# Three steps of the mixers issued later, six small tables loaded through GpSimd's queue

## The chip, the cores and the metric

One core of one Trainium2 chip runs the whole program in one launch. The metric is device time in microseconds, the median of repeated runs. TensorE (PE) does the matrix products, VectorE (DVE) and ScalarE (ACT) the elementwise work, GpSimd (POOL) a smaller share of it; SyncE (SP) issues nearly all the loads.

## What is computed

A decoder trunk of two layers over 256 positions of width 1024, in float32. Each layer runs four causal token mixers (retention, Mamba-2 SSD, gated linear attention, mLSTM) on the same normalised input, whose inputs all come from one wide projection. The four results are gated, merged and projected back. Then comes a channel mixer: a dense SwiGLU in layer 0, two of eight experts in layer 1.

```python
for l in range(DEPTH):
    h = rmsnorm(x, mix_norm_g[l])
    x = x + token_mixers(h, pos, w_in[l], ...)      # four mixers, gates, merge, w_out
    h = rmsnorm(x, ffn_norm_g[l])
    x = x + (swiglu(h, w1, w3, w2) if l % 2 == 0 else moe_ffn(h, router_w, w1, w3, w2))
return rmsnorm(x, final_norm_g)

# in token_mixers
u = h @ w_in                                        # sz, sxbc, sdt, gq, gk, gv, ga, mqk, mv, mi, mf, ...
xbc = silu(causal_dwconv(sxbc, ssd_conv_w, ssd_conv_b))     # SSD: x, B, C after a convolution
dt = softplus(sdt + ssd_dt_bias); a = -exp(ssd_a_log)       # SSD: scores are C @ B^T times decays of dt * a
alpha_pre = ga @ gla_w_alpha + gla_b_alpha                  # GLA: the rate product
m_t = maximum(inter, max(dlog))                             # mLSTM: a running maximum of the gate sums
```

## The kernel before

**Weights and cuts.** Each weight is read from memory once, in loads of 1 MB that SP issues (`fetch`, L270). A load is cut in two halves; each half is split in a high part (ScalarE, `hi`, L296) and a low part (VectorE, `lo`, L297), and three float32r products per tile (L302 to L304, `mm3`) stand for one float32 product. A half of a load is 24 matmuls of 256 columns, or 12 of 512. TensorE can start on a half when its `lo` is done. The order of the loads in a mixer stage is: z with the narrow columns, three of SSD's `xbc`, two of mLSTM's `mqk`, two of `mv`, then GLA, retention, gates, branches and the output.

**Side chains.** Everything between the projections is written as Python generators (`Side`), one per chain: `narrow` (rates, cumulative sums and mLSTM's maximum), `gla_decays`, `ssd`, `mlstm` and so on. The kernel keeps a modelled clock, `now`, which each `mm3` moves on by about 322 ns. After each `mm3`, `tick` steps every chain that is due. `yield n` makes a chain due again 1500 * n ns later, `yield 0` 700 ns later. So a `yield` sets after how many projection matmuls the chain's next instructions are issued, on every engine that they use.

**Orders.** The emission gives the priority; the framework's own scheduler makes each engine's queue from it, and only in the first norm and the z load of layer 0 are VectorE and ScalarE held to the written order. An engine works its queue in order: a TensorE instruction that waits holds up every projection matmul behind it.

**The tables.** `load_tables` (L353) is called once, after the first three weight loads. SP loads constants (L356, L357), five row tables (L360 to L364), five tables of eight numbers broadcast to all partitions (`bc`, L367), `walpha` (L369) and the router weights (L375). `ic`, `z` and `ea` in `narrow` (L677 to L686) read `bc`; GLA's rate product (L751) reads `walpha`.

**GLA's rate product.** `gla_decays` transposes its 16 narrow columns (L745), copies them out of PSUM (`gaT`, L748), multiplies by `walpha` (L751) and goes on to the decays; 9 us of the modelled clock after their scan it issues two exponentials on ScalarE (L776) over what GpSimd computes at L772 and L773.

**SSD.** `ssd` waits in emission for the convolutions of `xbc2` and `xbc4` (their last instruction is L578) and then issues the score products (L522, L523 from L980).

**mLSTM's maximum.** `narrow` scans the rows on VectorE (`mrow`, L726) and transposes the result on TensorE (L730).

**After the mixers.** Layer 0's SwiGLU follows in the same manner. Layer 1 ends with the experts, whose weights are loaded in 2 MB pieces (`quad`, L265) into buffers that exist only when the mixers' buffers have been given back.

Of the kernel before, what the change touches and what calls it, by code (L numbers as in the profile page):

```python
# [23 lines left out]
L = 2  # L24
# [78 lines left out]
def _bcast(ap, dims):  # L103

    return bass.AP(tensor=ap.tensor, offset=ap.offset, ap=[[0, P]] + dims)
# [36 lines left out]
class Trunk:  # L142
# [210 lines left out]
    def load_tables(self):  # L353
        nc, a = self.nc, self.a
        n0 = C_OFFS["ident"][1]
        nc.sync.dma_start(self.keep[:, n0:], a["consts"][:, n0:C_KEEP])  # L356
        nc.sync.dma_start(self.mixk[:, :C_LATE - C_KEEP], a["consts"][:, C_KEEP:C_LATE])  # L357
        rows = self.mixc.tile([102, P], F32, name="rows")
        r = lambda n, pat: a[n].rearrange(pat, p=P)
        nc.sync.dma_start(rows[0:48], r("ssd_conv_w", "l k (b p) -> (l k b) p"))  # L360
        nc.sync.dma_start(rows[48:60], r("ssd_conv_b", "l (b p) -> (l b) p"))
        nc.sync.dma_start(rows[60:92], r("ml_conv_w", "l k (b p) -> (l k b) p"))
        nc.sync.dma_start(rows[92:100], r("ml_conv_b", "l (b p) -> (l b) p"))
        nc.sync.dma_start(rows[100:102], r("gla_b_alpha", "l (b p) -> (l b) p"))  # L364
        self.bc = self.mixc.tile([P, 5, L, 4], F32, name="bc")
        for i, n in enumerate(("ssd_dt_bias", "ml_b_i", "ml_b_f", "ssd_a_log", "ssd_d")):
            nc.sync.dma_start(self.bc[:, i], _bcast(a[n], [[4, L], [1, 4]]))  # L367
        self.walpha = self.mixc.tile([16, L, P], F32, name="walpha")
        nc.sync.dma_start(self.walpha, a["gla_w_alpha"].rearrange("l r c -> r l c"))  # L369
        self.rows = rows  # L370
        self.ranks = self.const.tile([P, 2 * P], F32R, name="ranks")
        for i, n in enumerate(("tris", "ones")):
            nc.gpsimd.tensor_scalar(self.ranks[:, i * P:(i + 1) * P], self.c(n), 1.0, None, op0=OP.mult)
        self.rw = self.const.tile([P, KT, NE], F32, name="rw")
        nc.sync.dma_start(self.rw, a["router_w"][0].rearrange("(k p) e -> p k e", p=P))  # L375
# [205 lines left out]
    def mixers(self, l):  # L581
        nc, a, tc = self.nc, self.a, self.tc
# [19 lines left out]
        def wait(name):  # L602

            while name not in sides or not sides[name].done:
                yield 1
# [40 lines left out]
        def out_tile():  # L646
            po = self.psum()
            return po.rearrange("p (t h d) -> p t h d", t=2, h=4)
# [13 lines left out]
        def narrow():  # L662
# [7 lines left out]
            if l == 0:  # L670
                self.turn_tables()
            add_side("gla", gla_decays())
            for t in range(2):
                yield from silu2(szs[:, t], pz[t][:, :256])
# [49 lines left out]
            crow, mrow = [T((4, S), n_, 2, tag="row") for n_ in ("crow", "mrow")]  # L724
            nc.vector.tensor_copy(crow, pr[:4, :S])
            nc.vector.tensor_tensor_scan(mrow, crow, crow, 0.0, op0=OP.max, op1=OP.max)  # L726
            yield 1
            pm = self.psum()
            for t in range(2):
                nc.tensor.transpose(pm[:, t * 4:t * 4 + 4], mrow[:, t * P:(t + 1) * P], ident[:4, :4])  # L730
# [9 lines left out]
        def gla_decays():  # L740

            sm = G["sm"]
            pga = self.psum()
            for t in range(2):
                nc.tensor.transpose(pga[:16, t * P:(t + 1) * P], sm[:, t, 12:28], ident)  # L745
            yield 1
            gaT = T((16, S), "gaT", 2, tag="row")
            nc.vector.tensor_copy(gaT, pga[:16, :S])  # L748
            yield 0
            pal = self.psum()  # L750
            nc.tensor.matmul(pal[:, :S], self.walpha[:, l], gaT, start=True, stop=True)  # L751
            yield 1
            gz, ge, gu = T((P, S), "gz"), T((P, S), "ge"), T((P, S), "gu")
            nb = self.nvec[:, l:l + 1]
            nc.vector.tensor_scalar(gz, pal[:, :S], -1.0, nb, op0=OP.mult, op1=OP.add)
            nc.scalar.activation(ge, gz, AF.Abs)
            nc.scalar.activation(ge, ge, AF.Exp, scale=-1.0)
            yield 0
            nc.vector.tensor_scalar(gu, ge, 1.0, None, op0=OP.add)
            nc.vector.scalar_tensor_tensor(ge, gu, -1.0, ge, op0=OP.add, op1=OP.subtract)  # L760
            nc.scalar.activation(gu, gu, AF.Ln)
            yield 2
            nc.vector.tensor_sub(gu, gu, ge)
            nc.vector.scalar_tensor_tensor(gu, gz, 0.0, gu, op0=OP.max, op1=OP.add)
            nc.vector.tensor_tensor_scan(gz, gu, gu, 0.0, op0=OP.add, op1=OP.bypass)
            G["E"] = E = self.block("E").rearrange("p (n s) -> p n s", s=S)
            for i, s in enumerate(LEVELS):
                gv = gz.rearrange("p (n u s) -> p n u s", u=2, s=s)
                ev = E[:, i].rearrange("p (n u s) -> p n u s", u=2, s=s)
                n = S // (2 * s)  # L770
                ref = gv[:, :, 0, s - 1:s].to_broadcast([P, n, s])
                nc.gpsimd.tensor_tensor(ev[:, :, 0], ref, gv[:, :, 0], op=OP.subtract)  # L772
                nc.gpsimd.tensor_tensor(ev[:, :, 1], gv[:, :, 1], ref, op=OP.subtract)  # L773
            yield 6
            for i in range(0, NL, 4):
                nc.scalar.activation(E[:, i:i + 4], E[:, i:i + 4], AF.Exp, scale=-1.0 / 16.0)  # L776
            yield from gla_scores()
# [184 lines left out]
        def ssd():  # L962
# [12 lines left out]
            nc.gpsimd.tensor_tensor(hv(xdx), hv(xs), bc[:, 4, l, None, :, None].to_broadcast([P, 2, 4, 64]), op=OP.mult)  # L975
            for n in ("xbc2", "xbc4"):
                yield from wait(n)
            o, late = out_tile(), None
            for g in range(2):
                sc = self.scores(xbc[:, 2 + g], xbc[:, 4 + g])  # L980
# [149 lines left out]
        if l == 0:  # L1130
            add(order.close)
        spawn("narrow", narrow)
        for b in (0, 2, 4):
            plan += self.proj_cm(w, C_XBC + b * P, hT, ssd_conv(b))
            if b == 0:
                spawn("ssd", ssd)
# [585 lines left out]
```

## Time and profile before

| what | value |
|---|---|
| runs | 1483.81, 1484.91, 1490.21 us; median 1484.91 |
| profiled execution | 1487.51 us, of which the span is 1485.4 us |
| PE busy | 1384.5 us, 93% of the span |
| PE weight loads | 901.3 us, 61% |
| DVE busy | 612.1 us, 41% |
| ACT busy | 534.7 us, 36% |
| POOL busy | 185.3 us, 12% |
| mean granted TensorE clock | 0.983 of full |
| read from memory | 400.39 MB |

The shares are means over stages that differ: up to about 749 us the core computes two mixer stages and a SwiGLU, after that it streams expert weights. A busy PE isn't PE at its peak. What a change in one stage is worth has to be read from that stage's windows, from the waits and from the timeline around them. Times in rows are microseconds from the span's start unless the row says ns; the last figure in brackets of a timeline row is the idle time before the instruction and what ended it.

### The profile page before, as it was taken

The page shows a single profiled execution, that of the slowest core. Times are in us where ns is not written, and L with a number is a line of the kernel's source. Part 1 is how long each engine was busy: PE and PEld are TensorE (multiplying, and loading weights), DVE is VectorE, ACT ScalarE, POOL GpSimd, SP SyncE. Part 2 cuts the span into 40 slices and gives each one's busy share as a digit, 9 for nine tenths or more (in the row PEclk, how much of TensorE's full clock was granted, in tenths as well). Part 3 has the DMA queues.
Part 4 walks back from the last instruction along what each step waited for, and adds up shares of the span by engine and source line. Part 5 has one row for each costly group of instructions (what it writes and reads, how often), then busy time and mean ns, then how long its engine had stood idle before and what let it go on. Part 6 is the DMA issues. An engine that isn't in the chain of part 4 may idle for free. (4 is left out here: it accounts for less than half of the span.)

```text
span 1485.4 us, 26500 instructions
## 1 busy us (share of the span) xinstructions
PE 1384.5 (93%) x11170; PEld 901.3 (61%) x11170; DVE 612.1 (41%) x1069; ACT 534.7 (36%) x717; POOL 185.3 (12%) x211
## 2 busy tenths in 40 slices
PE   7999999999999999999999999989889998988884
PEld 6888999799998978999974332322223222332221
DVE  5866555654446786565553121221112121212112
ACT  5643444444444643344422322222222222222112
POOL 0366211100000227323110000000000000000000
PEclk9999999999999999999989999999999999999997
DMA  8735366675551433635387999999999999999991
GB/s 251 254 114 156 114 199 208 201 239 189 191 178 57 157 123 105 199 114 182 102 317 279 409 409 408 399 401 408 408 408 408 409 408 408 401 398 408 408 398 64
DMA packets 182474, 404.43 MB, mean 272 GB/s; under 512 B 12470, under 2 KB 95804, under 8 KB 182076
## 3 DMA queue, kind: packets, MB, share of 16 engines
q1 hardware_dynamic: 181612, 400.34, 73.2%
q8 instruction: 93, 1.52, 0.4%
q10 hardware_dynamic: 720, 2.16, 0.4%
q14 instruction: 49, 0.40, 0.1%
HBM read 400.39 MB, written 2.10 MB: 271 GB/s over the span
## 5 line engine op out<-in xcount | busy, mean ns | idle before, releaser
L312 PE MATMUL ps<-quad,X 128*32 128x512 f32 (+1 forms) x3072 | 325.6, 559 | 29.4 <-DMA quad<-in_moe_w_dram 29.1
L297 DVE TENSOR_TENSOR lo<-raw,hi 128x1024 fp32r<-128x1024 f32 x222 | 277.3, 1254 | 167.1 <-ACT hi L296 166.8
L302 PE MATMUL ps<-hThi,hi 128*128 128x256 f32 x1120 | 319.7, 285 | 0.0
L304 PE MATMUL ps<-hTlo,hi 128*128 128x256 f32 x1120 | 314.9, 281 | 0.4 <-DVE hTlo L297 0.4
L303 PE MATMUL ps<-hThi,lo 128*128 128x256 f32 x1120 | 314.9, 281 | 0.0
L296 ACT ACTIVATE hi<-raw 128x1024 fp32r<-128x1024 f32 x222 | 232.9, 1056 | 205.2 <-PE ps L304 114.1
L1511 DVE COPY own<-quad 128x1024 f32 (+1 forms) x140 | 92.7, 663 | 505.6 <-DMA quad<-in_moe_w_dram 439.0
L1512 ACT ACTIVATE own<-quad 128x1024 f32 (+1 forms) x140 | 141.1, 1010 | 443.9 <-DMA quad<-in_moe_w_dram 380.5
L312 PEld LDWEIGHTS ps<-quad,X 128*32 128x32 f32 x3072 | 92.0, 109 | 232.4 <-issue 160.0
L302 PEld LDWEIGHTS ps<-hThi,hi 128*128 128x128 f32 x1120 | 212.4, 190 | 2.9 <-issue 0.7
L303 PEld LDWEIGHTS ps<-hThi,lo 128*128 128x128 f32 x1120 | 211.7, 189 | 0.6
L304 PEld LDWEIGHTS ps<-hTlo,hi 128*128 128x128 f32 x1120 | 211.6, 189 | 0.6 <-DVE hTlo L297 0.6
L312 PE MATMUL ps<-quad,gT 128*32 128x512 f32 x1408 | 160.5, 595 | 28.5 <-DMA quad<-in_moe_w_dram 27.9
L312 PEld LDWEIGHTS ps<-quad,gT 128*32 128x32 f32 x1408 | 41.6, 109 | 143.3 <-issue 84.4
L416 POOL TENSOR_TENSOR rstd<-rs,mhalf 128x1 f32<-128x1 f32 x10 | 5.5, 556 | 932.1 <-DVE rs L412 915.1
L312 PE MATMUL ps<-own,X 128*32 128x512 f32 (+1 forms) x768 | 93.5, 558 | 0.0
L1103 POOL TENSOR_TENSOR m<-m 128x512 f32<-128x512 f32 x16 | 34.8, 2173 | 152.2 <-DVE m L1101 144.8
L312 PEld LDWEIGHTS ps<-own,X 128*32 128x32 f32 x768 | 24.3, 110 | 46.7 <-issue 44.3
L302 PE MATMUL ps<-hi,hThi 128*128 128x512 f32 (+1 forms) x128 | 51.2, 402 | 0.2 <-ACT hi L296 0.2
L304 PE MATMUL ps<-lo,hThi 128*128 128x512 f32 (+1 forms) x128 | 47.9, 375 | 0.4 <-DVE lo L297 0.4
L303 PE MATMUL ps<-hi,hTlo 128*128 128x512 f32 (+1 forms) x128 | 48.2, 377 | 0.0
L312 PE MATMUL ps<-own,gT 128*32 128x512 f32 x352 | 45.9, 593 | 0.0
(332 smaller groups left out, 1483.1 us busy)
## 6 DMA issues: line engine op xcount, KB each, us to landing
quad<-in_moe_w_dram SPq DMA_DIRECT2D x108, 2048.0 KB, 21.3
raw<-in_w_in_dram SPq DMA_DIRECT2D x62, 1024.0 KB, 5.5
quad<-in_moe_w_dram SPq DMA_DIRECT2D x32, 1536.0 KB, 16.8
raw<-in_ffn_w_dram SPq DMA_DIRECT2D x33, 1024.0 KB, 5.3
raw<-in_w_branch_dram SPq DMA_DIRECT2D x8, 1024.0 KB, 5.3
raw<-in_w_out_dram SPq DMA_DIRECT2D x8, 1024.0 KB, 5.0
mixk<-in_consts_dram SPq DMA_DIRECT2D x1, 1536.0 KB, 14.9
x<-in_x_dram SPq DMA_DIRECT2D x2, 512.0 KB, 5.2
```

Of the source, the lines that this page charges most:

```text
L296: nc.scalar.activation(hi, src, AF.Copy)
L297: nc.vector.tensor_sub(lo, src, hi.bitcast(F32))
L302: mm(out, ah, bh, start=start, stop=False)
L303: mm(out, al, bh, start=False, stop=False)
L304: mm(out, ah, bl, start=False, stop=stop)
L312: ins = self.nc.tensor.matmul(outs[gs], a, b, start=start, stop=stop, tile_position=(0, SUB * g))
L416: nc.gpsimd.tensor_tensor(out, v, mh, op=OP.pow)
L1103: nc.gpsimd.tensor_tensor(m[:, 0:2], m[:, 0:2], m[:, 2:4], op=OP.add)
L1511: nc.vector.tensor_copy(own[:, 0:1, :n_], raw[:, bass.ds(v0, 1)])
L1512: nc.scalar.activation(own[:, 1:2, :n_], raw[:, bass.ds(v1, 1)], AF.Copy)
```

## The change

Six loads move from SP's queue to GpSimd's. Three `yield`s change: mLSTM's maximum is transposed one step (1.5 us of the modelled clock) later, GLA's rate product is issued 3.0 us instead of 0.7 us after the copy before it, and a new `yield 4` (6 us) stands between the last convolution of SSD and its scores. No arithmetic changes.

```diff
@@ load_tables
         for i, n in enumerate(("ssd_dt_bias", "ml_b_i", "ml_b_f", "ssd_a_log", "ssd_d")):
-            nc.sync.dma_start(self.bc[:, i], _bcast(a[n], [[4, L], [1, 4]]))
+            nc.gpsimd.dma_start(self.bc[:, i], _bcast(a[n], [[4, L], [1, 4]]))
         self.walpha = self.mixc.tile([16, L, P], F32, name="walpha")
-        nc.sync.dma_start(self.walpha, a["gla_w_alpha"].rearrange("l r c -> r l c"))
+        nc.gpsimd.dma_start(self.walpha, a["gla_w_alpha"].rearrange("l r c -> r l c"))
@@ narrow
             nc.vector.tensor_tensor_scan(mrow, crow, crow, 0.0, op0=OP.max, op1=OP.max)
-            yield 1
+            yield 2
             pm = self.psum()
@@ gla_decays
             nc.vector.tensor_copy(gaT, pga[:16, :S])
-            yield 0
+            yield 2
             pal = self.psum()
             nc.tensor.matmul(pal[:, :S], self.walpha[:, l], gaT, start=True, stop=True)
@@ ssd
             for n in ("xbc2", "xbc4"):
                 yield from wait(n)
+            yield 4
             o, late = out_tile(), None
```

## Rows read from the trace of the kernel before

**Rows 1.** Windows by stage: from:to, length, busy us of PE, PEld, DVE, ACT, POOL, clock, DMA share, GB/s

```profile
13.00:477.00 464.00, 454.06 (x3243) 424.36 (x3244) 279.12 (x415) 213.82 (x284) 88.42 (x94) 0.99 0.57 182
477.00:749.00 272.00, 265.11 (x1914) 248.62 (x1914) 173.21 (x309) 122.28 (x180) 88.29 (x93) 0.98 0.42 134
749.00:1470.00 721.00, 657.17 (x5990) 222.35 (x5988) 152.13 (x330) 192.08 (x242) 5.62 (x14) 0.99 0.98 388
```

**Rows 2.** Waits of PE, whole span: us in total, times, longest us

```profile
PE ps L312 <- DMA quad<-in_moe_w_dram: 57.0, 82, 1.8
...
PE ps L522 <- DVE xbc L578: 6.2, 2, 3.2
PE ps L751 <- DVE gaT L748: 3.1, 1, 3.1
...
PE ps L730 <- DVE mrow L726: 1.1, 2, 0.7
```

**Rows 3.** Timeline of ACT, DVE and PE, 24 to 33 us: start, duration, instruction

```profile
25.34 0.21 ACT L686 ACTIVATE ea<-bc 128x4 f32<-128x4 f32 x1 [4.76 <-DMA bc<-in_ssd_a_log_dram]
...
26.52 1.23 DVE L297 TENSOR_TENSOR lo<-raw,hi 128x1024 fp32r<-128x1024 f32 x1 [2.46 <-ACT hi L296]
...
28.23 0.41 DVE L748 COPY gaT<-ps 16x256 f32<-16x256 f32 x1
...
28.70 0.69 PE L751 MATMUL ps<-gaT,walpha 16*128 16x256 f32 x2 [3.13 <-DVE gaT L748]
...
32.00 1.06 ACT L296 ACTIVATE hi<-raw 128x1024 fp32r<-128x1024 f32 x1 [3.27 <-DMA raw<-in_w_in_dram]
```

**Rows 4.** Timeline of SP's queue, start of the program

```profile
3.15 4.84 SPq L382 DMA_DIRECT2D narrow<-in_w_in_dram  x1
...
19.43 0.36 SPq L367 DMA_DIRECT2D bc<-in_ssd_dt_bias_dram  x1
...
22.03 0.43 SPq L369 DMA_DIRECT2D walpha<-in_gla_w_alpha_dram  x1
...
23.59 8.28 SPq L270 DMA_DIRECT2D raw<-in_w_in_dram  x4
```

**Rows 5.** Windows of a few us, columns as in rows 1

```profile
29.63:33.05 3.42, 3.42 (x18) 3.42 (x17) 2.35 (x13) 1.05 (x2) 0.00 (x0) 0.50 1.09 348
60.35:63.77 3.42, 3.42 (x12) 2.95 (x12) 2.78 (x7) 0.69 (x2) 0.00 (x0) 0.50 0.94 289
524.57:531.39 6.82, 5.67 (x16) 4.76 (x17) 6.12 (x12) 2.68 (x5) 0.00 (x0) 0.50 0.49 154
20.00:25.50 5.50, 5.50 (x47) 5.34 (x46) 2.07 (x7) 0.74 (x3) 1.06 (x2) 1.00 0.07 9
34.00:48.00 14.00, 13.53 (x113) 13.11 (x112) 14.00 (x35) 10.01 (x15) 6.41 (x9) 1.00 1.07 367
```

**Rows 6.** Timeline of ACT, DVE and PE ahead of SSD's scores, layers 0 and 1

```profile
47.95 1.06 ACT L776 ACTIVATE E<-E 128x1024 f32<-128x1024 f32 x1 [3.36 <-POOL E L773]
...
58.33 1.20 DVE L297 TENSOR_TENSOR lo<-raw,hi 128x1024 fp32r<-128x1024 f32 x1
59.46 0.67 DVE L578 SCALAR_TENSOR_TENSOR xbc<-th,xbc 128x512 f32<-128x512 f32 x1
...
60.28 1.13 PE L522 MATMUL ps<-xbc 128*128 128x256 f32 x2 [2.99 <-DVE xbc L578]
...
523.76 1.22 DVE L297 TENSOR_TENSOR lo<-raw,hi 128x1024 fp32r<-128x1024 f32 x1
...
525.73 1.19 PE L522 MATMUL ps<-xbc 128*128 128x256 f32 x2 [3.21 <-DVE xbc L578]
```

**Rows 7.** Timeline of POOL and DVE, start of the program

```profile
1.22 0.11 POOL L888 MEMSET mvv<- 128x16 f32 x1
6.83 0.55 POOL L416 TENSOR_TENSOR rstd<-rs,mhalf 128x1 f32<-128x1 f32 x1 [5.50 <-DVE rs L412]
...
8.14 1.41 DVE L442 SCALAR_TENSOR_TENSOR h<-x,rstd,gain_mix_norm_g 128x512 f32<-128x512 f32 x2 [1.45 <-DMA gain_mix_norm_g<-in_mix_norm_g_dram]
```

## The prediction, made before the changed kernel was run

> **What bounds the kernel now.** I read the windows by stage first. Up to 749 us TensorE is busy nearly all the time (454.1 of 464 us, then 265.1 of 272) while the DMA engines are at 0.57 and 0.42; after it they are at 0.98 and TensorE waits for expert weights [rows 1]. The expert stage starts when the last mixer buffers are free, and its loads set its length; so it keeps its length and moves as a block, and a microsecond that TensorE saves before 749 us should reach the end whole.
>
> Second, TensorE's waits [rows 2]. The 57.0 us for `quad` are the expert stage. What the change can touch is the scores of SSD (6.2 us, once per layer), GLA's rate product (3.1 us, layer 0 alone) and the transpose of mLSTM's maximum (1.1 us over both layers). Third, the timeline around each wait, for who is late, and fourth, short windows behind it for the granted clock.
>
> **What a wait costs besides its length.** Behind the rate product the clock is granted at 0.50, the 1.2 GHz level, for 3.42 us of full work; behind layer 0's scores for 3.42 us; in layer 1 the half-clock stretch runs to 531.39, and TensorE works in it from 525.73 [rows 5, 6]. Before each of them TensorE had stood still for about 3 us. Half of 3.42, 3.42 and 5.66 us are lost: 1.7, 1.7 and 2.8. The two waits for the maximum are short, and I give them no clock loss.
>
> **Part 1, the rate product and the tables.** The chain in layer 0 reads: `ea` on ScalarE waits 4.76 us for a table that SP issued late, the split of a weight half queued behind it starts only then, its `lo` on VectorE at 26.52, `gaT` at 28.23, and L751 on TensorE at 28.70 after 3.13 us idle, with all projection matmuls behind it [rows 3]. Either edit alone cuts this chain. The tables have no input to wait for, so GpSimd, idle from 1.33 to 6.83 us [rows 7], can issue them at once; and L751 comes 2.3 us of the modelled clock later, some 7 `mm3`. Gain: 3.1 + 1.7 = **4.8 us**.
>
> What is late next? The next load must be there. SP issues six tables, the router weights and a gain from 19.43 to 23.59, and then the next four loads [rows 4], while the DMA engines are at 0.07 [rows 5]. Six eighths of these 4.16 us are 3.1 us. The first of the four lands at 32.00, where ScalarE waits for it [rows 3], so then at 28.9; with the split (1.06) and `lo` (1.23) the half is ready at 31.2. TensorE, freed at 25.57, has the rate product (0.6 us) and 48 matmuls at 0.117 us (47 in 5.5 us [rows 5]), 5.6 us, and asks at 31.8: no wait.
>
> On the price of the six tables on SP, the Trainium skill (DMA: Bandwidth & Descriptors, "Issuing engines are not separate DMA queues") says that DMAs of all issuers run on the same 16 engines, and that another issuer saves only the time of issuing. By that, with 0.36 to 0.43 us for each issue [rows 4], the loads would come about 2.4 us earlier instead of 3.1, and the forecast would rise by 0.7; the gaps between these issues speak for the larger figure.
>
> **Cost at the start.** No row shows a DMA issued by GpSimd. Its queue also holds the power (`rstd`, 6.83) of the first norm, and VectorE and TensorE wait for that norm; behind it `h` waits for its gain until 8.14 anyway, 0.76 us after `rstd` ends [rows 7]. So six issues cost nothing if they end by 7.59, that is, up to 1.04 us each. Lower end: 0.36 us each as on SP, cost 0. Upper end: 4.84 us each, the dearest issue on SP [rows 4]: 29.0 us, so `rstd` at 30.4, and 22.8 us lost. No gain is possible here, since x and the gain are what is waited for. These loads are small like the 0.36 us row, so I stay near it, with a margin: 1.13 us each, **0.5 us** lost.
>
> **Part 2, the scores.** The last convolution instruction ends at 60.13, 2.8 us after TensorE ran out at 57.29 [rows 6]. Four steps are 6 us of the modelled clock, 18.6 `mm3`, 56 matmuls, 6.5 us at 0.117. That is twice the wait, in both layers. Gain: 3.0 + 1.7 in layer 0 and 3.2 + 2.8 in layer 1, **10.7 us**. What covers it: the matmuls that move ahead of the scores are those of `mv`, and their halves must be cut by then. Layer 0: TensorE would reach `mv` at 57.3 - 4.8 - 0.5 = 52.0 and its second half one half later (24 matmuls, 2.8 us), at 54.8. That half's `lo` ends at 59.53 [rows 6]. VectorE is busy for all of 34 to 48 us [rows 5], so its work moves up only as far as its start does; I give it the 3.1 us of the loads: 56.4, and TensorE waits 1.6 us. Between 0 (VectorE also gains from the moved scores) and 4.7 (all that was to be won) I take **1.6**. Layer 1: TensorE reaches `mv` 0.65 us earlier than 522.5 and wants its second half at 524.7; the `lo` ends at 524.98 [rows 6], 0.3 us late. But GLA's exponentials, which hold ScalarE up (3.36 us in layer 0 [rows 6]), come up to 2.3 us later too; they may fall behind the splits that they now delay, or delay them longer. Between 0 and 6.0 I take **1.0**. SSD's later steps end before retention's loads force them.
>
> **Part 3, the maximum.** One step is 1.5 us, the waits are 1.1 us in all [rows 2]: gain **1.1 us**. Its reader, mLSTM, waits for `mv` much longer.
>
> **Sum.** 4.8 + 10.7 + 1.1 = 16.6 us won; 0.5 + 1.6 + 1.0 = 3.1 given back; 13.5 net. The profiled execution takes 1487.5 us, 2.1 of them outside its span of 1485.4; it would come to 1474.0. The runs' median is 1484.9, 2.6 below that execution, so I forecast 1484.9 - 13.5 = **1471.4 us**.
>
> **Rivals.**
> *The cuts become the bound.* VectorE was full for 14 us at a stretch [rows 5]; what waited for the scores would wait for `lo` instead, as long and with the same clock loss. The 10.7 us go, 4.8 + 1.1 - 0.5 = 5.4 stay: 1479.5 us. Against it: 0.3 us is all that layer 1 shows.
> *The scores don't move on TensorE.* The `yield`s set the emission, the framework sets the queues; it may put the scores back where they were. Part 1 alone stays, 4.8 - 0.5: 1480.6 us. Against it: these queues follow the emission at every wait in rows 2.
> *The tables come late.* If GpSimd issues them only while VectorE is busy and is slowed by it, `ea` still holds ScalarE and TensorE then waits for the half behind it. Part 1 goes: 1476.2 us. VectorE's first instruction comes after 6 us and GpSimd is free from 1.33 [rows 7], which speaks against it.
> This is the rule in the Trainium skill, SBUF — State Buffer, "SBUF: two separate sides": GpSimd writes the descriptors of its DMAs itself and can't while certain VectorE instructions hold the port that both share. No run so far shows it.
> *Slower: the norm waits behind the tables.* At 4.84 us for each issue the 22.8 us of above are lost at `rstd`, and 1484.9 - 14.0 + 22.8 = 1493.7 us. It decides against the change from (14.0 + 0.76 + 5.50) / 6 = 3.4 us per issue on, nine times the SP row.
>
> **How the numbers follow.** Forecast 0.65 (its own range 1467 to 1477), cuts 0.12, scores don't move 0.10, tables late 0.08, slower 0.05. The low end, 1467, is nearly all of the 16.6 us with 1 us for luck; the high end, 1480, takes in the tables' case and most of the cuts'. About 0.5%, 7.4 us, is what a measurement of this kernel can tell from no change. Faster by more (under 1477.5): 0.63 of the forecast, 0.06 of the tables' case, 0.04 of the cuts': 0.73. Within: 0.21. Slower by more: 0.06, the slow rival and a little for what I don't see.
>
> **What would show it.** Right: no wait at L751, L522 from `xbc` and L730; full clock at 25 to 36, 55 to 66 and 520 to 534 us; the four loads issued at about 20.5; `rstd` before 8 us; the first `quad` load some 13 us earlier, and the expert stage as long as before. A row that waits for `lo` or `hi` in 45 to 60 or 520 to 530 would size parts 1 and 2; `ea` still waiting, the tables' case. Wrong would be an expert stage that takes back what was won, or a first TensorE product of the z load after 15 us.

## The result, and the profile of the changed kernel

The changed kernel takes **1492.97 us** (median of 11 runs, 1491.42 to 1496.26); the kernel before takes 1484.15 (11 runs beside them). The ratio is 1.0058, with a 95% interval of 1.0045 to 1.0070: slower by 0.6%, where 1471.4 and a range of 1467 to 1480 stood in the forecast. The profiled execution takes 1493.46 us with a span of 1491.3. From L978 on, lines of the changed kernel stand one higher than before; L442 to L842, which are named most, are the same lines.

The waits of TensorE over the whole span come first (us in total, times, longest), beside [rows 2]:

```profile
...
PE ps L452 <- DVE h L442: 13.2, 4, 9.0
PE ps L842 <- POOL bd L827: 5.3, 2, 2.8
PE ps L522 <- DVE xbc L578: 2.7, 2, 2.2
PE ps L710 <- issue: 2.7, 1, 2.7
PE ps L531 <- DVE as L988: 1.8, 2, 1.1
...
PE ps L802 <- POOL ge L791: 0.6, 1, 0.6
...
PE ps L730 <- DVE mrow L726: 0.3, 1, 0.3
```

The three waits that the change aimed at are nearly gone: L751 from 3.1 us to none, L522 from 6.2 to 2.7, L730 from 1.1 to 0.3. In their place stand 9.0 us at L452, the first norm's transposes; 2.7 at L710, the sums of the rates; 5.3 at L842, GLA's products, which wait for a masked copy (`bd`) made by GpSimd; and smaller ones at L531 and L802. So 7.4 us of waits went, and some 15 came (L452 had 7.4 us before, L842 1.1). The page names no releaser for L710. Its operand is `rates`, whose last write on VectorE ends just ahead of it:

```profile
40.50 0.17 DVE L705 COPY rates<-sp 128x8 f32<-128x8 f32 x1
...
40.77 0.36 PE L710 MATMUL ps<-rates,mixk 128*128 128x8 f32 x2 [2.73 <-issue]
```

The start, from the timelines of GpSimd, ScalarE, SP's queue and TensorE:

```profile
1.31 0.80 POOL L367 DMA_DIRECT2D bc<-in_ssd_dt_bias_dram  x1
...
4.22 0.56 POOL L369 DMA_DIRECT2D walpha<-in_gla_w_alpha_dram  x1
...
12.84 0.57 POOL L416 TENSOR_TENSOR rstd<-rs,mhalf 128x1 f32<-128x1 f32 x1 [7.94 <-DVE rs L412]
...
11.48 0.20 ACT L686 ACTIVATE ea<-bc 128x4 f32<-128x4 f32 x1 [5.54 <-DMA bc<-in_ssd_a_log_dram]
11.60 0.61 ACT L421 ACTIVATE junk<-x 128x512 bf16<-128x512 f32 x1
...
4.08 7.34 SPq L382 DMA_DIRECT2D narrow<-in_w_in_dram  x1
...
24.30 8.41 SPq L270 DMA_DIRECT2D raw<-in_w_in_dram  x4
...
14.25 1.97 PE L452 MATMUL ps<-keep,h 128*128 128x128 f32 x8 [8.99 <-DVE h L442]
```

GpSimd's issues are cheap, 0.56 to 0.80 us, and over by 4.8. But the framework has now put `ea`, which stood at 25.34 before [rows 3], between the squares of `x` on ScalarE, and there it waits until its table lands, 8.3 us after that table's issue. The written order to which ScalarE is held at the start begins behind these squares, which are emitted with the load of `x`, and ends ahead of `ea`; so it doesn't keep the two apart. `rstd` therefore comes at 12.84 instead of 6.83 [rows 7], and not for the reason that the slower rival gave, since GpSimd's issues were over 8 us earlier. SP's second narrow load needs 7.34 us where it needed 4.84 [rows 4]. In spite of six issues less, the four loads go out at 24.30, not at 20.5 and not even at 23.59.

The half-clock stretches of the mixers (columns as in rows 1: from:to, length, busy us of PE, PEld, DVE, ACT, POOL, clock, DMA share, GB/s):

```profile
7.70:17.90 10.20, 3.29 (x14) 2.89 (x15) 4.07 (x10) 4.50 (x12) 1.12 (x2) 0.50 0.83 175
41.84:45.25 3.41, 3.41 (x18) 3.41 (x17) 3.41 (x10) 3.12 (x5) 0.00 (x0) 0.50 0.98 359
96.45:99.86 3.41, 3.41 (x9) 2.76 (x9) 1.10 (x3) 0.15 (x1) 2.27 (x5) 0.50 0.00 0
120.34:123.75 3.41, 3.20 (x11) 2.85 (x11) 1.12 (x5) 0.00 (x0) 2.05 (x5) 0.50 0.00 0
488.98:492.39 3.41, 3.41 (x16) 3.41 (x17) 3.03 (x5) 1.74 (x3) 0.00 (x0) 0.50 0.51 155
```

The clock is at 0.50, the 1.2 GHz level, in each. Those at 29.63 and 60.35 [rows 5] are gone; others stand behind the new waits, at L710 (41.84), L802 (96.45) and L842 (120.34). The one at 488.98 follows the norm of layer 1, as one does in the kernel before (clock 0.53 from 480.40 to 483.80). Not every stop has one: behind L842's 2.8 us in layer 1, which end at 589.09, the clock is 1.00.

To see where time comes and goes, I take the start of TensorE's n-th projection matmul (L302 to L304, the same 4584 in every kernel) minus its start in the kernel before. Numbers 330 and 3330 come behind both groups of SSD's scores, in layer 0 and in layer 1, in every kernel; 480 and 624 lie behind mLSTM's and behind GLA's heads of layer 0; the last is the end of the mixers. The rows below that of after are kernels of the experiments; VectorE stands for eight of GLA's products moved to it.

```
matmul no.          0    192    330    384    480    624   3168   3330   3384   3552   last
before, us       13.2   44.5   75.9   84.9  108.9  145.9  513.8  550.7  568.4  608.5  748.2
after            +4.9   +4.8   +0.1   +1.5   +4.1   +7.2   +5.8   +3.5   +5.8   +7.7   +7.7
tables only      +4.4   +1.8   +3.9   +3.9   +3.9   +3.9   +3.8   +4.1   +4.1   +4.0   +4.0
scores only       0.0   +2.3   -4.4   -3.0   +1.4   +1.4   +1.7   -3.6   +2.4   +2.6   +2.6
scores + VectorE +0.1   +2.7   -4.1   -2.7   -2.6   -2.6   -3.5   -8.8   -8.1   -8.1   -8.1
VectorE only     -0.1   +2.7   -0.9   -0.9   -0.9   -0.9   -0.2   -1.3   -1.3   -1.3   -1.3
rate step only   -0.1   +0.2   +2.9   +2.9   +5.5   +8.3   +5.6   +7.4   +7.7   +8.9   +8.9
```

In the row of after, the start loses 4.9; TensorE wins 4.7 in layer 0 (from 192 to 330) and 2.3 in layer 1 (3168 to 3330); and then all of it is given back, and more, in the heads that follow (330 to 624, and 3330 to 3552). The experiments take these three apart.

A profile is one execution, and two of the same code can differ by some microseconds: the profiled one of the kernel before stands 2.6 above its median. The expert stage, from the last mixer product to the end, takes 735.4 us in after (1491.3 - 755.9) against 737.2, and between 732.9 and 739.3 over all kernels of this document. So the table shows where time goes; what an edit costs is taken from the medians.

### The profile page after: what moved, and what is told of

It is laid out like the page before. It is cut to its first block, busy times and chain, and to the rows that moved or that the text cites. A ratio compares the mean times of both kernels' runs of the same rounds, so it can differ in the third digit from the quotient of the medians.

```text
span 1491.3 us, 26537 instructions
## 1 busy us (share of the span) xinstructions
PE 1381.7 (93%) x11170; PEld 897.8 (60%) x11170; DVE 609.6 (41%) x1069; ACT 534.5 (36%) x717; POOL 185.5 (12%) x217
## 5 line engine op out<-in xcount | busy, mean ns | idle before, releaser
L302 PE MATMUL ps<-hThi,hi 128*128 128x256 f32 x1120 | 320.0, 286 | 0.0
L304 PE MATMUL ps<-hTlo,hi 128*128 128x256 f32 x1120 | 315.0, 281 | 0.4 <-DVE hTlo L297 0.4
L302 PEld LDWEIGHTS ps<-hThi,hi 128*128 128x128 f32 x1120 | 212.6, 190 | 3.0 <-issue 0.7
L304 PEld LDWEIGHTS ps<-hTlo,hi 128*128 128x128 f32 x1120 | 211.8, 189 | 0.6 <-DVE hTlo L297 0.6
L302 PE MATMUL ps<-hi,hThi 128*128 128x512 f32 (+1 forms) x128 | 51.1, 401 | 0.0
L304 PE MATMUL ps<-lo,hThi 128*128 128x512 f32 (+1 forms) x128 | 48.0, 376 | 0.8 <-DVE lo L297 0.8
```

What stands on the lines that cost most here:

```text
L302: mm(out, ah, bh, start=start, stop=False)
L304: mm(out, ah, bl, start=False, stop=stop)
```

## Experiments

Times are medians; the ratio is to the kernel before, run beside the others on the same chip. Its medians there were 1485.44, 1486.27, 1486.04, 1485.20 and 1485.14 us.

### The change in halves

Tables only:

```diff
-            nc.sync.dma_start(self.bc[:, i], ...)
+            nc.gpsimd.dma_start(self.bc[:, i], ...)
-        nc.sync.dma_start(self.walpha, ...)
+        nc.gpsimd.dma_start(self.walpha, ...)
```

> The six tables go through GpSimd's queue, the three yields are as before. Theory (the table loads delay the start: ScalarE's exponential of ssd_a_log now stands ahead of the squares of x and waits for its table): the first transposes of the norm start at about 14 us instead of 8.9, five us are lost there, the 3.1 us wait at the rate product and its clock loss come back, and the time is 1484 to 1490 us. Rival (the tables help, the moved steps are what costs): no loss at the start beyond 1 us, about 1480 us.

Measured: 1490.57 us, 1.0031 [1.0019, 1.0042]. The first projection product is 4.4 us late; `ea` ends its wait at 10.87. L751's wait is gone, yet the scores' waits grew from 6.2 to 8.2 us and the mixers end 4.0 late. The theory had the place right, and the time is just above its range.

Steps only (`yield 2` for the maximum, `yield 2` for the rate product, `yield 4` for the scores; tables on SP):

> The three yields as after, the tables on SP's queue as before. Theory: the start is that of the kernel before (first transposes at 8.9 us), the rate product's wait still goes, and what the moved scores win is given back at the GLA products that wait for GpSimd: 1480 to 1486 us, five to ten us less than after. Rival (the tables cost nothing, the steps do): 1490 us or more.

Measured: 1491.64 us, 1.0036 [1.0020, 1.0051], the rival's time. The start is as before. L751's wait is gone too, and L710 waits 3.2 us at 36.88 instead. So either half loses by itself, and both parts of the forecast were wrong.

### The start: which of the tables' effects costs it

After, with `ssd_a_log` alone back on SP, so that `ea` waits for no late table:

```diff
-            nc.gpsimd.dma_start(self.bc[:, i], ...)
+            q = nc.sync if n == "ssd_a_log" else nc.gpsimd
+            q.dma_start(self.bc[:, i], ...)
```

> As after, but ssd_a_log alone is loaded through SP again; the other five tables stay with GpSimd. Theory (the exponential ahead of the squares): ScalarE's squares run as before, the first transposes start before 10 us, and about five us of the loss at the start go: 1487 to 1489 us. Rival (loads through GpSimd slow the DMA engines for everyone): the second and third weight load still start at about 14 us and most of the five us stay: 1491 to 1494 us.

Measured: 1492.74 us, 1.0049 [1.0031, 1.0067], the rival's time. `ea` no longer stands ahead of the squares, and the first transposes start at 9.16, as before. But the first product still comes 2.8 us late, for its weights: the first half of the first projection weight is split at 11.29 in the trace before, without a wait for its load; here the rows of SP's queue and of ScalarE read

```profile
3.00 7.97 SPq L383 DMA_DIRECT2D narrow<-in_w_in_dram  x1
...
13.82 1.06 ACT L296 ACTIVATE hi<-raw 128x1024 fp32r<-128x1024 f32 x1 [2.06 <-DMA raw<-in_w_in_dram]
```

The tables that still come through GpSimd make SP's narrow load 3.1 us longer and the weight late. The converse, before with `ssd_a_log` alone on GpSimd:

```diff
-            nc.sync.dma_start(self.bc[:, i], ...)
+            q = nc.gpsimd if n == "ssd_a_log" else nc.sync
+            q.dma_start(self.bc[:, i], ...)
```

> Before with one edit: only the table ssd_a_log loads through GpSimd's queue, the other five through SyncE. In this order ea stands ahead of all of x's squares on ScalarE. Theory A (a place of ea ahead of the squares makes the first norm wait for that table's landing, 5 to 8 us after its issue at 1.3 us; few packets slow the loads little): SyncE's second narrow load under 6 us, the first product 1 to 3 us late if the table lands at 7 to 9 us, 1486 to 1489 us. Rival B (it is the number of packets alone): the first product at 13.2 us, 1485 us.

Measured: 1486.15 us, 1.0004 [0.9995, 1.0013]. ScalarE's timeline, then SP's queue:

```profile
7.70 0.20 ACT L687 ACTIVATE ea<-bc 128x4 f32<-128x4 f32 x1 [4.76 <-DMA bc<-in_ssd_a_log_dram]
7.81 0.61 ACT L422 ACTIVATE junk<-x 128x512 bf16<-128x512 f32 x1
```

`ea` stands ahead of all four squares and holds them until 7.81; with one table of six, SP's narrow load takes 4.40 us. The first product is 2.0 us late. So both effects exist: the other tables alone cost the first product 2.8 us, `ea`'s place with its one table 2.0. In after they don't follow one another. There the weight is waited for no more (its split at 16.75 follows its predecessor without idle time), and the norm's transposes, 5.3 us late, account for the 4.9 by themselves. The other tables act through `ea`: its table is the fourth to be issued, at 3.17 instead of 1.29, and needs 8.3 us to land instead of 6.4. This kernel's last product is only 0.2 us late, though: a delay ahead of the scores can shorten their wait (L523, the same line one higher, waits 1.1 instead of 3.0 in layer 0), so the start's loss and the scores' gain don't add up.

If packets on the way at the start are the trouble, the tables could go later. First held until the constants have landed:

```diff
+        nc.gpsimd.tensor_scalar(self.bc..., self.c("ones")..., 1.0, None, op0=OP.mult)
+        nc.gpsimd.tensor_scalar(self.walpha..., self.c("ones")..., 1.0, None, op0=OP.mult)
+        nc.gpsimd.dma_start(...)   # the six tables
```

> Before with the six tables on GpSimd's queue, but held until the constants have landed (GpSimd first writes the two tiles from the constants, about 14 us), so that none is on the way while the first weights load. No step is moved. Theory A (the start is lost to the tables' packets between 3 and 12 us, and to ea standing ahead of x's squares): the first product starts at 13.2 us as before, SyncE's second narrow load takes 4.8 us again, raw4 is issued at 20.5 us instead of 23.6, its hi comes at 29 us, the waits of L751 and L710 are under 1.5 us together, and the time is 1481 us (1478 to 1483). Rival B (raw4's landing is set by the DMA engines, not by its issue): raw4 is issued early but lands at 32 us as before, 1485 us (1483 to 1487). Rival C (tables from GpSimd are late wherever they stand): ea or sm's additions wait, start as before, 1487 to 1490 us.

Measured: 1493.11 us, 1.0045 [1.0028, 1.0062]. From SP's queue, ScalarE and TensorE:

```profile
3.04 4.89 SPq L384 DMA_DIRECT2D narrow<-in_w_in_dram  x1
...
20.54 8.36 SPq L270 DMA_DIRECT2D raw<-in_w_in_dram  x4
...
31.48 0.20 ACT L688 ACTIVATE ea<-bc 128x4 f32<-128x4 f32 x1 [11.06 <-DMA bc<-in_ssd_a_log_dram]
...
34.88 1.19 PE L753 MATMUL ps<-gaT,walpha 16*128 16x256 f32 x2 [8.41 <-DVE sA L692]
```

The start is the old one, and the four loads go out at 20.54, the very time of the forecast: that step of it was right. But GpSimd saw the constants only at 19.86, its transfers landed 5.2 to 8.5 us after their issue at 22.4 to 25.3, and now `ea` and the whole narrow chain are late (rival C, with 3 us more than it said). So a third place, right behind the second `rstd`:

```diff
+            if l == 0:
+                self.load_small(h)   # writes both tiles from h, then the six DMAs on GpSimd
```

> Before with the six tables on GpSimd's queue, issued after both inverse roots of the first norm (about 11 to 15 us, held by writes from h), and no step moved; ea keeps its place behind the first four cuts. With the tables at 22 us raw4 was issued at 20.5 us as forecast, but TensorE waited 8.4 us at L751 for the narrow chain, whose tables landed 5.2 to 8.5 us after their issue. Theory A (GpSimd's transfers need 5 to 8.5 us wherever they stand; in the gap between the first loads and the narrow chain they fit): first product at 13.2 us, raw4 issued at 20.5 to 21.5, tables landed by 23, wait at L751 under 1 us, raw4's hi at 29 to 30 and L710's wait under 1.5 us: 1480 to 1483 us. Rival B (their packets slow the loads that are on the way then, raw2 and raw3 and the constants): these land 2 to 4 us later, the first 96 products end as late as 25 to 28 us, 1486 to 1490 us.

Measured: 1489.89 us, 1.0024 [1.0010, 1.0039], rival B. The tables are issued from 12.8 to 16.3 us. The rate product waits for nothing any more, and `ea`, which waits 3.5 us for its table where it waited 4.76, keeps nobody waiting; but SP, which before a further issue waits for an earlier weight to land, waits 5.2 us for it. Its waits, in this kernel and then in the one before:

```profile
SPq L372 <- DMA raw<-in_w_in_dram: 5.2, 1, 5.2
```

```profile
SPq L367 <- DMA raw<-in_w_in_dram: 2.7, 1, 2.7
```

The four loads go out at 23.88, and TensorE waits 4.3 us for the rates. At each of three places in time the six tables cost more than their issue on SP did.

### The scores

The `yield 4` alone, all else as before:

```diff
+            yield 4
             o, late = out_tile(), None
```

> Only the yield 4 ahead of SSD's scores; all else as before. Theory (the scores' wait goes, but SSD's tail falls into GLA's work on GpSimd): no wait of 3 us at the scores, waits of 2 us and more at the GLA products in both layers, and a time within 4 us of before, 1481 to 1488. Rival (the forecast's: the 10.7 us of the scores come through to the end but for about 2.6): 1476 us.

Measured: 1488.83 us, 1.0022 [1.0010, 1.0033]. The wait is won (-6.7 from matmul 192 to 330, -5.3 from 3168 to 3330) and lost again behind it, +4.5 close to 100 us and +5.7 at 563. I had expected waits at GLA's products; the longest is at L637, which transposes a mixer's result. What stands there in layer 1, from the timelines of GpSimd, VectorE and TensorE:

```profile
556.05 3.49 POOL L796 TENSOR_TENSOR E<-gqk,E 128x128 f32<-128x128 f32 x8
...
560.06 0.70 POOL L416 TENSOR_TENSOR srr<-rs,mhalf 128x2 f32<-128x2 f32 x1
...
556.37 0.17 DVE L412 TENSOR_SCALAR rs<-sss 128x2 f32<-128x2 f32 x1 [4.67 <-ACT xdx L1002]
560.80 0.88 DVE L1007 SCALAR_TENSOR_TENSOR Y<-xs,srr,hg 128x256 f32<-128x256 f32 x2 [4.26 <-POOL srr L416]
...
563.43 0.63 PE L637 MATMUL ps<-keep,Y 128*128 128x128 f32 x4 [2.17 <-DVE am L934]
```

and the window behind it:

```profile
563.43:570.25 6.82, 6.82 (x24) 5.34 (x25) 5.88 (x12) 2.86 (x5) 4.32 (x6) 0.57 0.50 156
```

`rs` is ready at 556.5, but SSD's inverse root (`srr`) stands in GpSimd's queue behind eight of GLA's products and a masked copy; VectorE, whose next instruction needs it, stands 4.26 us; what is queued behind that reaches TensorE late; and TensorE goes on at a clock of 0.57. In layer 0 the same wait of VectorE is 4.86 us long. In the kernel before, `srr` stood ahead of GLA's products; GpSimd's timeline in layer 0:

```profile
82.27 0.73 POOL L416 TENSOR_TENSOR srr<-rs,mhalf 128x2 f32<-128x2 f32 x1 [1.57 <-DVE rs L412]
85.54 4.01 POOL L797 TENSOR_TENSOR E<-gqk,E 128x128 f32<-128x128 f32 x7 [2.54 <-ACT gqk L783]
```

If the order of this queue is what costs, a smaller step, which leaves `srr` in its place, should keep the gain.

```diff
+            yield 2      (and, in the second kernel, yield 3)
             o, late = out_tile(), None
```

> Before with one edit: the SSD scores come two steps later instead of four. In this order the SSD's inverse root (srr, L416 on GpSimd) stands ahead of GLA's first product on GpSimd's queue, as it did before; with four steps it stood behind 16 products and two or three masked copies. Theory A (the gain of the moved scores is given back because srr then waits 4.1 to 4.9 us in GpSimd's queue, after which TensorE waits at L637 and falls to half clock): srr follows rs within 1.6 us in both layers, no wait over 1 us at L637, and most of the 5.6 us per layer of the scores stays: 1478 us (1475 to 1481). Rival B (whatever comes later in the SSD chain comes back at the chain's end, through its own length): the wait is as with four steps or smaller by half, the give-back likewise, 1485 to 1488 us.

> Before with one edit: the SSD scores come three steps later. In this order srr stands behind GLA's first products in part (one in layer 0, 0.5 us). Theory A: as with two steps, 1478 us (1475 to 1482), the scores' wait shorter still than with two and srr at most 1 us late in layer 0. Rival B: between two and four steps, 1486 to 1489 us.

Measured: 1486.40 us, 0.9999 [0.9984, 1.0013], and 1486.31, 0.9998 [0.9986, 1.0011]. `srr` isn't late in either, and there is no wait at L637; but there is no gain to keep, since L522 still waits 3.0 to 3.3 us. Up to three steps the framework leaves the first scores where they were, in layer 0 behind 288 projection matmuls, and moves only the second group (from behind 300 to 312 and 318); four steps put the first behind 297 and the second behind 327. The rival that the scores don't move holds below four, for the first, which are those that wait; these two runs say nothing on the give-back. So take the suspected cause away, with four steps kept:

```diff
-                nc.gpsimd.tensor_tensor(ev[:, :, 0], kv[:, :, 0], ev[:, :, 0], op=OP.mult)
```

> Scores four steps later, as in the run with that edit alone (1488.8 us), and eight of GLA's sixteen products on GpSimd (the first halves of E times k, 3.5 us per layer) left out, so that the output differs; the order of everything else on GpSimd is the same, with srr still behind the other eight and the masked copies. Theory A: srr follows rs within 1 us, the 2.2 us wait at L637 of layer 1 and the half clock behind it (3.5 us) go, and the 4.5 us of layer 0 too: 1479 us (1476 to 1482). Rival B: the give-back stays, 1486 to 1489 us.

Measured: 1478.08 us, 0.9936 [0.9918, 0.9953]. `srr` now stands at 552.54 with `rs` at 552.16, the half clock near 100 and near 565 us is gone, and the mixers end 7.1 us early. The kernel can have that without leaving work out, since VectorE has room at that point:

```diff
-                nc.gpsimd.tensor_tensor(ev[:, :, 0], kv[:, :, 0], ev[:, :, 0], op=OP.mult)
+                nc.vector.tensor_tensor(ev[:, :, 0], kv[:, :, 0], ev[:, :, 0], op=OP.mult)
```

> Scores four steps later, nothing of the tables, and the eight products that the last run left out are made by VectorE instead of GpSimd, so that nothing is missing from the output. GpSimd's order is that of the run with the half products. Theory A (GpSimd's queue in front of srr is what gives the scores' gain back, not the products as such): as with the products left out, srr within 1.5 us of rs, no wait over 1 us at L637, no half clock at 97 to 105 us nor at 563 to 573 us: 1479 us (1476 to 1482), a kernel that is faster than both. Rival B (VectorE's queue takes GpSimd's place, eight products of some 0.25 us before the decays and lo): waits of 2 us or more at L522, L531 or L637 again, 1484 to 1489 us.

Measured: **1476.13 us, 0.9927 [0.9906, 0.9949]**, faster than both kernels. GpSimd and VectorE in layer 1, then the window that was at 0.57:

```profile
551.23 0.61 POOL L827 TENSOR_TENSOR bd<-E,mixk 128x256 f32<-128x256 f32 x1
551.94 0.70 POOL L416 TENSOR_TENSOR srr<-rs,mhalf 128x2 f32<-128x2 f32 x1
...
545.63 5.05 DVE L796 TENSOR_TENSOR E<-gqk,E 128x128 f32<-128x128 f32 x8
...
551.50 0.36 DVE L412 TENSOR_SCALAR rs<-sss 128x2 f32<-128x2 f32 x1 [0.17 <-ACT xdx L1002]
...
563.00:569.80 6.80, 6.80 (x59) 6.75 (x58) 2.89 (x9) 3.72 (x9) 4.06 (x5) 1.00 0.50 154
```

The eight products take 5.05 us on VectorE, more than on GpSimd (3.49 in the kernel with the scores alone), but behind them, up to 620 us, TensorE waits for nothing longer than 0.5 us. Is it the split that wins? The same edit without the scores' move:

> Before with one edit: the eight products made by VectorE instead of GpSimd, scores and everything else where they were. Theory A (in before no wait of TensorE hangs on those products, since srr stands ahead of them; the run that was faster owes its 10 us to the scores' move, which the split only keeps): the scores wait 3 us in both layers as before, 1485 us (1483 to 1487). Rival B (the split is a gain of its own, GpSimd being the bound of GLA's part): 1476 to 1480 us.

Measured: 1484.04 us, 0.9995 [0.9985, 1.0006]: nothing. The split only keeps what the scores' move wins. But the scores of layer 0 don't wait 3 us as before. TensorE's waits up to 140 us:

```profile
PE ps L710 <- issue: 3.0, 1, 3.0
PE ps L522 <- DVE xbc L578: 1.6, 1, 1.6
...
PE ps L751 <- DVE gaT L748: 0.4, 1, 0.4
```

Nothing is changed ahead of these waits: up to 45 us every engine has the order of the kernel before. Yet L751 waits 0.4 us instead of 3.1, L710 waits 3.0 instead of not at all, and TensorE comes some 2 us later to the scores, whose wait is the shorter for it. The profiles of the kernels with three and with four steps, with half the products and with the divided ones show the same exchange (L751 0.4 to 1.6, L710 2.1 to 3.2); those with two steps or with the maximum alone don't (3.2 and 3.3 at L751). Either `ea`'s table had landed 2.6 us after its issue instead of 4.2 (the three kernels with half or divided products), or the half clock at the start had lasted longer (three and four steps). Whether that differs by kernel or by execution, no run tells. So a part of what the table shows as won in layer 0 is no effect of the scores' move: against the kernel with the split alone, the fast kernel is 1.8 us ahead at matmul 384, and 6.8 at the last.

### The rate product and the maximum

Both, with scores and tables as before:

```diff
-            yield 1      (ahead of mLSTM's maximum)
+            yield 2
-            yield 0      (ahead of GLA's rate product)
+            yield 2
```

> Before with two edits: GLA's rate product and mLSTM's maximum come two steps later; scores and tables as before. Theory A (raw4's landing is the bound; the wait only moves): L751's wait of 3.1 us goes, L710 waits 2 to 3.5 us some 8 us later with half clock behind it, the 192nd product is within 2.5 us of before's, and the end of the mixers within 1.5 us: 1486 us (1484 to 1489). The forecast's own step: 4.8 us at L751 and 1.1 at the maximum won, 1480 us.

Measured: 1494.72 us, 1.0051 [1.0031, 1.0070], worse than either theory. One at a time:

> Before with one edit: GLA's rate product comes two steps later. In this order GLA's fourth masked copy (bd_3, L827) stands behind mLSTM's product on GpSimd (L555, 2.2 us), where before had it ahead. Theory A (that place costs, the wait at L751 only moves): L842 waits 2.0 to 2.8 us for bd in both layers with half clock behind it, L802 may wait for ge, L751's wait goes and L710's comes; 1490 to 1495 us, about all that the run with rate product and maximum lost (8.7 us). Rival B (the maximum lost it): 1484 to 1487 us and no wait at L842 over 1 us.

> Before with one edit: mLSTM's maximum comes two steps later. GpSimd's order is as before (bd_3 ahead of L555, srr ahead of GLA's products). Theory A: L730's 0.5 us wait goes, nothing else: 1485 us (1484 to 1487). The forecast's step: 1.1 us won, 1485. Rival B (it is the maximum that costs): waits at the scores of 4 us and more, 1490 us and over.

Measured: the rate step 1490.78 us, 1.0039 [1.0023, 1.0054], in theory A's range; the maximum 1487.79, 1.0015 [1.0007, 1.0024], between theory and rival. TensorE's waits in the kernel with the rate step alone:

```profile
PE ps L522 <- DVE xbc L578: 8.7, 2, 4.7
...
PE ps L842 <- POOL bd L827: 4.1, 2, 2.0
PE ps L710 <- issue: 2.4, 1, 2.4
```

and, from the timelines of ScalarE, VectorE and GpSimd in layer 0:

```profile
53.90 1.06 ACT L776 ACTIVATE E<-E 128x1024 f32<-128x1024 f32 x1 [3.07 <-POOL E L773]
56.85 1.06 ACT L776 ACTIVATE E<-E 128x1024 f32<-128x1024 f32 x1 [1.89 <-POOL E L773]
...
58.85 0.48 DVE L572 SCALAR_TENSOR_TENSOR mqk<-ps,vec,mqk 128x255 f32<-128x255 f32 x1 [5.05 <-ACT mqk L565]
...
117.74 2.19 POOL L555 TENSOR_TENSOR Y<-sq,gsm 128x512 f32<-128x512 f32 x1 [1.14 <-DVE sq L554]
119.89 3.30 POOL L827 TENSOR_TENSOR bd<-E,mixk 128x256 f32<-128x256 f32 x4
```

Two things can be read there. GLA's differences on GpSimd come later, so the exponentials, which already waited 3.36 us on ScalarE [rows 6], now hold it until 57.9; the convolution's pieces queued behind them reach VectorE late, and the scores wait 4.7 us instead of 3.0. And the fourth masked copy, which GpSimd made at 111.07 before, ahead of mLSTM's product L555, now stands behind it: L842 waits 2.0 us, in both layers. That the rate step costs is shown; no run takes either of the two away, so what each costs isn't. The maximum costs in another way: its own wait is gone in the mixers, but the scores come earlier (behind 283 matmuls in layer 0, where it was 288) and wait 3.4 and 4.7 us. In its profile the mixers end only 0.5 us late, so that the 2.6 us of the medians come from there is argued, not shown.

### After, with the products divided

After as it is, with the edit of the fast kernel (eight products on VectorE):

> After, whole, with one edit: eight of GLA's sixteen products are made by VectorE instead of GpSimd, as in the run that was faster. srr then stands behind eight products less; bd_3 still stands behind L555, and the tables still load through GpSimd. Theory A (in after the start gives 5 us to the tables, and most of what the scores win is lost in GpSimd's queue): srr within 2 us of rs, the start 4 to 5 us later than before, L842 still waits 2 us in each layer or less: 1486 us (1483 to 1489), 4 to 10 us less than after. Rival B (after's loss is not GpSimd's queue): 1491 to 1494 us.

Measured: 1491.36 us, 1.0031 [1.0013, 1.0048]; less than after by about a quarter of a per cent, and above the 1483 to 1489 that I expected. `srr` no longer keeps anybody waiting, but 4.2 us at the start, 2.4 at L710 and 2.0 us in each layer at L842 remain. The scores' give-back is only one of after's three losses.

## Why the prediction was wrong, point by point

The steps that failed, in the forecast's own terms: SSD's tail, priced at nothing, took back all that the scores won (the scores alone lose 3.4 us where 8.1 net stood); the start, priced at 0.5 us, cost 4.9; and the moved rate product, a gain of 4.8, cost 5.6.

- **What bounds the kernel, and what a wait costs: right in the main.** Time lost or won in the mixers reaches the end: in the fast kernel the expert stage takes 737.0 us (1477.1 - 740.1), against 737.2. But it isn't as fixed as the forecast has it (732.9 to 739.3 us). Half clock mostly follows the stops and costs about as much again; the 5.7 us at 563 in the kernel with the scores alone are 2.2 of wait and 3.5 of half clock.
- **Start, 0.5 us: wrong by 4.4.** The price of an issue was bounded well (0.56 to 0.80 us, where I took 1.13). The step that failed is that nothing but the issues was priced. I moved six DMAs and forgot the reader: `ea` has no other input, and the framework put it ahead of the norm's squares, presumably because it takes the table to be ready early; so the table's landing entered the norm's chain. And I gave the packets no price on the DMA engines, which were busy with the first weights. The Trainium skill (DMA: Bandwidth & Descriptors, "Issuing engines are not separate DMA queues"), cited in the forecast, says that DMAs of all issuers share 16 engines and that another issuer saves only issue time; the runs agree with the first half (SP's narrow load took 7.34 us instead of 4.84 beside the six tables), and the saving of issue time was real once (20.54), yet it was never kept.
- **Part 1, 4.8 us at L751: wrong.** "No wait" came true, but I asked only whether the next half would be there for the matmuls. The next thing on TensorE that waits for the narrow chain is L710, whose rates go through a long run of small VectorE instructions behind the cuts: 2.7 us in after, 2.4 with the rate step alone. And the wait at L751 isn't the fixed cost that one trace made it: in five kernels that leave the start alone it is 0.4 to 1.6 us, and L710 takes 2.1 to 3.2 there too. So the 4.8 us couldn't be counted on. And of the moved step I counted only its matmul: GLA's whole chain behind it, GpSimd's differences, ScalarE's exponentials and the masked copies, moved too. The step alone costs 5.6 us (1490.78 - 1485.20).
- **Part 2, 10.7 us at the scores: near in size once GpSimd's queue is relieved, wrong in what is late next.** Then 9.9 us are measured (1486.04 - 1476.13). That is luck in part: of the 8.1 us by which that profile's mixers end earlier, 1.3 come with the split alone, and layer 0 gives 1.8 us where 4.7 stood. I had said that "SSD's later steps end before retention's loads force them", and so gave the tail no price; it is the step that failed. In GpSimd's queue the tail met GLA's products, and VectorE stood 9.1 us behind them (4.86 and 4.26). The cover that I looked for, and charged with 2.6 us, was VectorE's `lo`; no wait for `lo` is above 0.8 us in after. The conversion of four steps into 56 matmuls was wrong as well: the first scores moved by 9, the second group by 27. Nine at 0.117 us are 1.1 us, which leaves a wait of 1.1 to 2.2 us in layer 1; in layer 0 it is nearly gone because TensorE also comes later there (column 192 of the table).
- **Part 3, 1.1 us: wrong in sign.** The wait went, and the time grew by 2.6 us (1487.79 - 1485.20). The scores, which now came 5 to 8 matmuls earlier, wait 2.0 us more (8.2 against 6.2); where the rest is, isn't shown.
- **Rivals.** None held as told. "Slower, the norm waits behind the tables" has the right victim and the wrong queue: `rstd` waited for ScalarE's squares, not for GpSimd's issues, and came 6.0 us later, not 22.8. "The tables come late" happened in substance (8.3 us from issue to landing), but the rule that I gave it, GpSimd kept from writing descriptors by VectorE, isn't what was seen: VectorE's first instruction in after is at 12.3 us, when the last table, issued at 4.22, had needed 8.1 us to land. "The scores don't move" holds for the first scores at two or three steps.

What stays open: why the packets of a few small tables hold up the large loads. The runs show that they do, at the start (the first weight's split 2.5 us later) and at 13 to 22 us (SP's wait 5.2 us instead of 2.7), and no run tells whether it is their number, their size or their place on the engines. Why the whole loses less (8.8 us) than its halves together (5.1 and 6.2), or than its four edits one by one (5.1, 3.4, 5.6 and 2.6), was not taken further apart.

## What to carry to other kernels

Before moving a step, follow it to its last instruction on every queue and read who stands next to whom there afterwards; an engine that is idle most of the time can still become the bound, when the order of its queue puts long work ahead of a short step that others wait for. Where a move wins at its own place and loses behind it, look for the two instructions that changed places, and take one of them to another engine: here eight products on VectorE turned +0.2% into -0.7%. A load that is moved to another queue has a landing time and a reader, and both move with it. And a wait that one trace shows should be looked for in a second one before it is priced.

## What the runs showed of the hardware

The tables were slow to land from GpSimd's queue, however cheap their issue was. From the DMA part of the page (KB each, us from issue to landing), first after:

```profile
bc<-in_ssd_a_log_dram POOLq DMA_DIRECT2D x1, 4.0 KB, 8.3
...
walpha<-in_gla_w_alpha_dram POOLq DMA_DIRECT2D x1, 16.0 KB, 8.1
```

then before, where SP issued them, and last a row table that SP loads among the first weights:

```profile
walpha<-in_gla_w_alpha_dram SPq DMA_DIRECT2D x1, 16.0 KB, 5.2
...
rows<-in_ml_conv_w_dram SPq DMA_DIRECT2D x1, 16.0 KB, 6.0
```

The queue is not shown to be the cause. SP issued the tables while the DMA engines were at 0.28 (19 to 23 us); GpSimd's were on their way at 0.92 to 1.04, at the start, at 13 and at 22 us alike, and SP's own small load, issued at 15.16 and on its way at 0.86 (up to 21.20), took 6.0 us as well. No run has the tables of either queue in the other's traffic.

The Trainium skill (DMA: Bandwidth & Descriptors, "Anatomy of one DMA — SWDGE (gpsimd) path") gives a transfer on this path about 2.0 us and its bytes' time; here it was 5.1 to 8.6 us, so beside other loads the measurement decides.

The half clock at the very start is not a fixed cost. With the same code and order there, it covers about 3.4 us in some kernels' executions (before, at 9.11 to 12.52; clock 0.51) and up to some 10 us in others (scores only: 0.84, 0.50, 0.50 and 0.65 in the four slices of 3.41 us from 5.70 on), and the 48th product then comes 1.8 us later. A difference of that size at the start of two profiles can't be put down to an edit by itself.
